# A two-layer hybrid decoder step on one core: the norm's first step on ScalarE, mixer B's affine step on GpSimd, eight logit tiles in place of ten

## The chip, the core and the metric

The kernel runs on one core of a Trainium2 chip. A core has five engines with a queue of instructions each: TensorE (PE, with its weight loads shown apart as PEld), VectorE (DVE), ScalarE (ACT), GpSimd (POOL) and SyncE (SP), which here issues the DMA transfers. The engines wait for one another by semaphores; within a queue the order is fixed when the program is built. The metric is the device time of one execution in microseconds (us); less is better.

## What is computed

One inference step of a decoder trunk of two layers, for a prompt of 2048 tokens (model width 1024) and for eight sample tokens that attend to 2048 cached tokens each. All is in float32. Layer 0 runs a chunked spatial gate (mixer A) and stick-breaking attention (mixer B, 8 heads of 64); layer 1 runs sparse softmax attention with 256 selected keys per query and a relative bias (mixer C, 8 query heads, 2 key heads) and causal pooling (mixer D). Each layer has one input projection, one output projection and a norm behind it:

```python
def stick_breaking(q, k, v, q_pos, k_pos):
    z = jnp.einsum('bqhd,bkhd->bhqk', q.astype(jnp.float32), k.astype(jnp.float32)) * HEAD_DIM ** -0.5
    mask = k_pos[None, :] < q_pos[:, None]
    log_keep = jnp.where(mask, jax.nn.log_sigmoid(-z), 0.0)
    later = lax.cumsum(log_keep, axis=3, reverse=True) - log_keep
    att = jnp.where(mask, jnp.exp(jax.nn.log_sigmoid(z) + later), 0.0)
    return jnp.einsum('bhqk,bkhd->bqhd', att, v.astype(jnp.float32)).astype(v.dtype)
...
    logits = jnp.where(valid[:, :, None, None, :], logits + bias, -jnp.inf)
    p = jax.nn.softmax(logits, axis=-1)
    o = jnp.einsum('bqgrk,bqkgd->bqgrd', p, v_sel)
...
def _layer_norm(x, g, b):
    return (_standardize(x) * g.astype(jnp.float32) + b.astype(jnp.float32)).astype(x.dtype)
...
def post_norm(x, h, w_o, g, b):
    return _layer_norm(DN_ALPHA * x + jnp.einsum('bte,ed->btd', h, w_o), g, b)
```

The outputs are both token groups behind layer 1, and the new keys, values and pooling rows of both layers.

## The kernel before

**Tiling.** The prompt is cut into four blocks of 512 tokens (i, or the block's number), each block into four tiles of 128 tokens, one per partition. Keys come in pieces of 512 columns (TB). A projection is computed in three float32r matmuls of split operands: wh and wl are a weight's high and low halves (L475 on ScalarE, L478 on GpSimd or VectorE), xh and xl those of the input (L462 on ScalarE, L468 on VectorE or GpSimd).

**Mixer B** goes block by block: for a pair of heads m, a key piece s and each head a of the pair, `b_logits` makes four tiles of 128 queries by up to 512 keys: the logits z (L839, TensorE), the keep probability by a sigmoid, the mask on the diagonal piece (L849, GpSimd), and a running product over the keys from the right (L853, a scan on VectorE). `b_values` transposes them (L876), copies them (L877, ScalarE) and multiplies with the values (L885). While the last block (i = 3) runs beside mixer C, the sigmoid is written as 0.5 + 0.5 tanh (`self.exp`: mixer C's exps use ScalarE too): L843 is the tanh, L844 the affine step. These are 4 pairs x 4 pieces x 2 heads x 4 tiles = 128 steps, 104 of them 128x512 and 24 of fewer columns on the diagonal.

**The norm** (`ln`) follows the output projection of each block and layer: statistics and a reciprocal square root by small steps on VectorE (rs_t at L492 to L495 is part of it), ln_nb = -mean x ln_rs at L1017, and then for each half c of the 1024 columns and each of four token tiles three steps in place on the rows xres: x ln_rs + ln_nb (L1026), times g (L1027, GpSimd, lng), plus b (L1028, VectorE, lnb). A norm of a block has eight such triples of 128x512; that of the sample tokens has two of 8x512. Behind layer 0 the rows are stored, loaded again, transposed on TensorE (ps_x), and split into xh and xl for layer 1's projection (pp at L549 to L551).

**Mixer C** goes by query tiles j = 0 to 15; tile j has j + 1 key tiles of 128, that is 1 to 4 pieces. For each head `c_logits` loads a bias tile nm and adds the mask to it (L1568, GpSimd), multiplies (z_c, L1581) and evicts each piece with mask and row maximum (L1583, VectorE) into a tile zt of the pool "z"; L1587 takes the maximum of the pieces (nmax). `c_values` takes the exp (L1599, ScalarE), transposes (L1612), copies (L1614, ScalarE) and, for two heads together, multiplies with the values (av_c, L1626). A counter z_free lets c_logits begin a piece only when a tile is free; L1626's loop frees two at a time. The tokens' selection (tk_ names) runs on VectorE, ScalarE and GpSimd. The sample tokens' work (names with s_) runs in the background.

**Stages.** `run` opens three sets of tile pools, one after the other. In the trace they take 0 to 1310 us (layer 0 and most of mixer B), 1310 to 1990 us (mixer B's last block beside mixer C's first tiles; here self.exp holds), and 1990 to 2925 us (mixer C's tiles 8 to 15 and three output projections with their norms); the last norms fill the tail to 2963 us. `BUFS_C` sizes the pools of the last stage.

**What sets the order.** The program is first written as streams that are woven together, and then the class `Order` plans it anew: a list scheduler over all instructions, with a cost for each by engine, operation and shape, with semaphore and transfer delays, and with the number of tiles of each tag as a limit. It plans three times (by program order, then by the latest start in the plan before) and keeps the plan with the shortest estimate. So an edit to an engine or a buffer count re-orders every queue, not only the lines edited.

## Time and profile before

| | us |
|---|---|
| median of three runs | 2964.18 |
| lowest, highest | 2955.64, 2974.54 |
| the profiled execution | 2964.62 |
| its span in the trace | 2962.9 |
| TensorE busy in the span | 2747.0 |
| VectorE busy | 2163.9 |
| ScalarE busy | 1561.7 |
| GpSimd busy | 1112.2 |

TensorE's granted clock over the whole span is 0.96 of full speed; full speed is 2.4 GHz and the lower level 1.2 GHz. The engines work beside each other, so the busy times do not add up to the span. An idle time in the rows below is that of the engine named, just before the instruction, with the engine and line that released it.

### The profile page before, as it was taken

To read this page: it belongs to the slowest core of one execution; us is meant where nothing else is said; L and a number is where in the kernel's file an instruction comes from. 1 tells how busy PE (TensorE), PEld (TensorE's weight loads), DVE (VectorE), ACT (ScalarE), POOL (GpSimd) and SP (SyncE) were. 2 spreads that over 40 slices of the span, in tenths; PEclk is the share of its full clock that TensorE was granted. 3 is DMA by queue.
4 is the path that set the end of the run, shared out by engine and by line. 5 is a ranking of instruction groups with operands and counts; after the bars stand their busy time and mean duration, and the time that the engine had idled before them with its cause. 6 is when DMAs were issued, how large, how long until landed. Compare 5 with 4: busy or idle time off the path is not lost. (4 is left out here: it accounts for less than half of the span.)

```text
span 2962.9 us, 52295 instructions
## 1 busy us (share of the span) xinstructions
PE 2747.0 (93%) x17490; PEld 2184.8 (74%) x17490; DVE 2163.9 (73%) x5493; ACT 1561.7 (53%) x3148; POOL 1112.2 (38%) x1172
## 2 busy tenths in 40 slices
PE   7998999989999999979799999998899998998995
PEld 6886777767767777768477677777777887887885
DVE  2366557856775887438988998897897778887766
ACT  2433333334444344435466677784577666675852
POOL 2323335423324543242433422335422555344342
PEclk9999999999999999989899999999999999998998
DMA  7566865776585668453665455425655565675452
GB/s 220 166 175 195 266 191 186 239 227 205 172 245 165 216 184 292 147 155 111 194 173 152 140 144 146 122 79 146 189 164 157 171 190 161 213 216 172 129 185 67
DMA packets 536594, 523.51 MB, mean 177 GB/s; under 512 B 43184, under 2 KB 408905, under 8 KB 536288
## 3 DMA queue, kind: packets, MB, share of 16 engines
q1 hardware_dynamic: 526439, 484.29, 55.1%
q0 software_dynamic: 9856, 35.66, 3.9%
q8 instruction: 138, 2.26, 0.3%
q14 instruction: 161, 1.31, 0.1%
HBM read 430.27 MB, written 89.73 MB: 176 GB/s over the span
## 5 line engine op out<-in xcount | busy, mean ns | idle before, releaser
L478 POOL TENSOR_TENSOR wl<-wr,wh 128x512 fp32r<-128x512 f32 x260 | 410.7, 1580 | 967.8 <-ACT wh L475 810.5
L549 PE MATMUL pp<-xh,wh 128*128 128x512 f32 (+1 forms) x1536 | 635.6, 417 | 10.2 <-DVE q_hl L468 6.1
L550 PE MATMUL pp<-xl,wh 128*128 128x512 f32 (+1 forms) x1536 | 616.4, 402 | 9.6 <-DVE rs_t L494 8.2
L551 PE MATMUL pp<-xh,wl 128*128 128x512 f32 (+1 forms) x1536 | 616.0, 401 | 1.0 <-DVE wl L478 1.0
L475 ACT CAST wh<-wr 128x1024 fp32r<-128x1024 f32 x260 | 269.9, 1038 | 386.5 <-PE pp L550 198.7
L478 DVE TENSOR_TENSOR wl<-wr,wh 128x512 fp32r<-128x512 f32 x260 | 219.0, 843 | 210.7 <-ACT wh L475 190.0
L549 PEld LDWEIGHTS pp<-xh,wh 128*128 128x128 f32 (+1 forms) x1536 | 288.6, 189 | 95.7 <-issue 27.8
L550 PEld LDWEIGHTS pp<-xl,wh 128*128 128x128 f32 (+1 forms) x1536 | 290.6, 189 | 68.6 <-issue 9.3
L551 PEld LDWEIGHTS pp<-xh,wl 128*128 128x128 f32 (+1 forms) x1536 | 289.6, 189 | 63.9 <-issue 4.6
L944 PE MATMUL pp_o<-wh,oh 128*128 128x256 f32 x1008 | 301.0, 300 | 17.9 <-ACT oh L462 11.8
L946 PE MATMUL pp_o<-wh,ol 128*128 128x256 f32 x1008 | 291.5, 293 | 2.6 <-POOL ol L468 2.6
L945 PE MATMUL pp_o<-wl,oh 128*128 128x256 f32 x1008 | 293.2, 292 | 0.0
L853 DVE TENSOR_TENSOR_SCAN P<-P,bfst 128x512 f32<-128x512 f32 x192 | 268.5, 1408 | 22.3 <-ACT P L846 21.8
L877 ACT COPY P<-ps_p 128x512 f32<-128x512 f32 (+1 forms) x320 | 166.0, 523 | 189.2 <-PE ps_p L876 180.4
L1581 PE MATMUL z_c<-ksc,qc 128*128 128x512 f32 (+3 forms) x816 | 222.0, 355 | 32.6 <-DVE mx L1583 27.3
L1599 ACT ACTIVATE zt<-zt,nmax 128x512 f32<-128x512 f32 (+3 forms) x320 | 209.0, 655 | 76.8 <-DVE nmax L1587 76.3
L1614 ACT COPY zt<-ps_pc 128x512 f32<-128x512 f32 (+3 forms) x320 | 164.1, 520 | 114.9 <-PE ps_pc L1612 113.3
L944 PEld LDWEIGHTS pp_o<-wh,oh 128*128 128x128 f32 x1008 | 198.1, 197 | 28.7 <-ACT oh L462 13.2
L1568 POOL TENSOR_TENSOR nm<-nm,mk 128x256 f32<-128x256 f32 (+1 forms) x128 | 92.7, 725 | 335.1 <-DMA nm<-bft 186.1
L839 PE MATMUL z<-ks,q 128*128 128x512 f32 (+3 forms) x640 | 194.0, 391 | 18.9 <-DMA ks<-ksc 10.8
L946 PEld LDWEIGHTS pp_o<-wh,ol 128*128 128x128 f32 x1008 | 197.1, 197 | 8.8 <-POOL ol L468 4.5
L945 PEld LDWEIGHTS pp_o<-wl,oh 128*128 128x128 f32 x1008 | 198.5, 197 | 5.2 <-issue 2.1
(456 smaller groups left out, 5861.2 us busy)
## 6 DMA issues: line engine op xcount, KB each, us to landing
pg<-cache_b_kv SPq DMA_DIRECT2D x256, 256.0 KB
wr<-w_in_even SPq DMA_DIRECT2D x112, 512.0 KB
wr<-w_in_odd SPq DMA_DIRECT2D x76, 512.0 KB
wr<-w_out SPq DMA_DIRECT2D x68, 512.0 KB
ks<-ksc SPq DMA_DIRECT2D x80, 256.0 KB
ksc<-kcs SPq DMA_DIRECT2D x80, 256.0 KB
q<-qsc SPq DMA_DIRECT2D x64, 256.0 KB
qc<-qcs SPq DMA_DIRECT2D x128, 128.0 KB
```

The source lines that it names most:

```text
L475: nc.scalar.copy(hi, raw)
L478: e.tensor_tensor(lo[:, c], raw[:, c], hi[:, c].bitcast(F32), op=OP.subtract)
L549: nc.tensor.matmul(ps[:m], wh[:, kt, :m], xh[kt], start=a, stop=False)
L550: nc.tensor.matmul(ps[:m], wh[:, kt, :m], xl[kt], start=False, stop=False)
L551: nc.tensor.matmul(ps[:m], wl[:, kt, :m], xh[kt], start=False, stop=b)
L839: nc.tensor.matmul(z[:, :n], q2[:, c, t * P:(t + 1) * P].bitcast(F32R), ks[:, :n].bitcast(F32R), start=c == 0, stop=c == 1)
L853: nc.vector.tensor_tensor_scan(r, r, r, initial=ini, op0=OP.mult, op1=OP.bypass)
L944: nc.tensor.matmul(ps[:, :256], oh[:, tt], wh[:, k], start=a, stop=False)
L945: nc.tensor.matmul(ps[:, :256], oh[:, tt], wl[:, k], start=False, stop=False)
L946: nc.tensor.matmul(ps[:, :256], ol[:, tt], wh[:, k], start=False, stop=b)
L1581: nc.tensor.matmul(z[:, :n], q2[:, c, jj % 2, :].bitcast(F32R), kk, start=c == 0, stop=c == 1)
L1599: nc.scalar.activation(zt, zt, AF.Exp, bias=nmx, accum_out=st["rs"][:, h, c:c + 1])
```

## The change

Three edits. `BUFS_C` gives mixer C's last phase eight logit tiles z where it had ten. The affine step behind the tanh (L844) goes from VectorE to GpSimd. The norm's first step (L1026) goes from VectorE to ScalarE, as an ACTIVATE of the identity with a scale and a bias per row, which computes the same.

```diff
@@ -37,7 +37,7 @@
 BUFS = {"tmp": 4, "tok": 4, "ot": 3, "hl": 1, "wr": 2}
 BUFS_A = {"P": 4, "q2": 3, "vs": 2}
 BUFS_M = {"P": 3, "q2": 2, "vs": 1, "z": 6, "kv": 2}
-BUFS_C = {"z": 10, "kv": 4}
+BUFS_C = {"z": 8, "kv": 4}
 KT = 8
 T = 2048
 TB = 512
@@ -841,7 +841,7 @@
             p = Ps[:, t]
             if self.exp:
                 nc.scalar.activation(p[:, :n], z[:, :n], AF.Tanh, scale=-0.0625)
-                nc.vector.tensor_scalar(p[:, :n], p[:, :n], 0.5, 0.5, op0=OP.mult, op1=OP.add)
+                nc.gpsimd.tensor_scalar(p[:, :n], p[:, :n], 0.5, 0.5, op0=OP.mult, op1=OP.add)
             else:
                 nc.scalar.activation(p[:, :n], z[:, :n], AF.Sigmoid, scale=-0.125)
             if diag:
@@ -1023,7 +1023,7 @@
             nc.sync.dma_start(b, self.bc(self.I["ln_b"][layer, cs], P))
             for t, y in enumerate(ys):
                 z = y[c]
-                nc.vector.tensor_scalar(z, z, rs[:n, t:t + 1], nb[:n, t:t + 1], op0=OP.mult, op1=OP.add)
+                nc.scalar.activation(z, z, AF.Identity, scale=rs[:n, t:t + 1], bias=nb[:n, t:t + 1])
                 nc.gpsimd.tensor_tensor(z, z, g[:n], op=OP.mult)
                 nc.vector.tensor_tensor(z, z, b[:n], op=OP.add)
             yield
```

In instructions that are 128 steps fewer on VectorE and more on GpSimd at L844, and 68 fewer on VectorE and more on ScalarE at L1026 (64 of 128x512, 4 of 8x512). TensorE's instructions are the same in number. The plan of every queue is new.

The first place is VectorE in the norm of block 2, layer 0: xres_15197 to xres_15203 are its four row tiles, rs_t and ln_rs of 8x1 belong to the sample tokens' norm, xl_16612 is the low half of the next projection's input. Before, on VectorE:

```order
L492 TENSOR_TENSOR rs_t_16553<-ln_rs_16551 8x1
L1026 TENSOR_SCALAR xres_15199<-xres_15199,ln_rs_16486,ln_nb_16504 128x512
L493 TENSOR_TENSOR rs_t_16553<-rs_t_16553,rs_a_16552 8x1
L1026 TENSOR_SCALAR xres_15201<-xres_15201,ln_rs_16486,ln_nb_16504 128x512
L494 TENSOR_SCALAR rs_t_16553<-rs_t_16553 8x1
L1028 TENSOR_TENSOR xres_15199<-xres_15199,lnb_16507 128x512
L495 TENSOR_TENSOR ln_rs_16551<-ln_rs_16551,rs_t_16553 8x1
L1026 TENSOR_SCALAR xres_15203<-xres_15203,ln_rs_16486,ln_nb_16504 128x512
L492 TENSOR_TENSOR rs_t_16553<-ln_rs_16551 8x1
L1028 TENSOR_TENSOR xres_15201<-xres_15201,lnb_16507 128x512
L493 TENSOR_TENSOR rs_t_16553<-rs_t_16553,rs_a_16552 8x1
L468 TENSOR_TENSOR xl_16612<-ps_x_16606,xh_16611 128x512
```

The last three of eight L1026 and two adds stand here ahead of xl.

Now, on VectorE, the same stretch up to the same xl (tk_ names belong to mixer C's selection):

```order
L1309 TENSOR_SCALAR tk_sd_16896<-tk_b_16898 128x1
L1382 TENSOR_SCALAR tk_b1_15964<-tk_tn_15706 128x1
L493 TENSOR_TENSOR rs_t_16553<-rs_t_16553,rs_a_16552 8x1
L1028 TENSOR_TENSOR xres_15199<-xres_15199,lnb_16507 128x512
L494 TENSOR_SCALAR rs_t_16553<-rs_t_16553 8x1
L1310 TENSOR_TENSOR tk_sd_16896<-tk_sd_16896,tk_a_16897 128x1
L495 TENSOR_TENSOR ln_rs_16551<-ln_rs_16551,rs_t_16553 8x1
L1028 TENSOR_TENSOR xres_15201<-xres_15201,lnb_16507 128x512
L492 TENSOR_TENSOR rs_t_16553<-ln_rs_16551 8x1
L1321 TENSOR_SCALAR tk_tt_16908<-tk_sd_16896,tkc_165,tk_mv_16895 128x1
L493 TENSOR_TENSOR rs_t_16553<-rs_t_16553,rs_a_16552 8x1
L468 TENSOR_TENSOR xl_16612<-ps_x_16606,xh_16611 128x512
```

The adds are left; small steps of the selection have moved in between them.

And on ScalarE, where the first steps now stand; xh_16611 is the high half that xl_16612 needs, P a copy of mixer B, zt an exp of mixer C:

```order
L1026 ACTIVATE xres_15197<-xres_15197,ln_nb_16504,ln_rs_16486 128x512
L1026 ACTIVATE xres_15199<-xres_15199,ln_nb_16504,ln_rs_16486 128x512
L1026 ACTIVATE xres_15201<-xres_15201,ln_nb_16504,ln_rs_16486 128x512
L877 COPY P_16195<-ps_p_16615 128x4x128
L1026 ACTIVATE xres_15203<-xres_15203,ln_nb_16504,ln_rs_16486 128x512
L462 CAST xh_16611<-ps_x_16606 128x512
L1649 ACTIVATE c_sum_16628<-ps_rb_16623 128x256
L1327 ACTIVATE mk_16645,tk_ss_16910<-ix_16644,tk_tt_16908 128x512
L1599 ACTIVATE zt_16639,rs_16330<-zt_16639,nmax_16782 128x256
```

The eight L1026 left VectorE's queue ahead of xl; on ScalarE all eight stand ahead of xh.

The second place is GpSimd ahead of the same norm: wl are low halves of weights, nm bias tiles of mixer C, P the probability tiles of mixer B. Before, on GpSimd:

```order
L478 TENSOR_TENSOR wl_16095<-wr_16092,wh_16094 128x512
L1568 TENSOR_TENSOR nm_16336<-nm_16336,mk_15227 128x256
L478 TENSOR_TENSOR wl_16149<-wr_16146,wh_16148 128x512
L1568 TENSOR_TENSOR nm_16635<-nm_16635,mk_15227 128x256
L1568 TENSOR_TENSOR nm_16787<-nm_16787,mk_15227 128x256
L478 TENSOR_TENSOR wl_16386<-wr_16383,wh_16385 128x144
L478 TENSOR_TENSOR wl_16455<-wr_16452,wh_16454 128x512
L1568 TENSOR_TENSOR nm_16973<-nm_16973,mk_15227 128x256
L1286 AFFINE_SELECT ix_16644<-ix_16644 128x128
L1568 TENSOR_TENSOR nm_17078<-nm_17078,mk_15227 128x256
```

Weight halves and bias tiles alternate. Now, on GpSimd:

```order
L478 TENSOR_TENSOR wl_16095<-wr_16092,wh_16094 128x512
L478 TENSOR_TENSOR wl_16149<-wr_16146,wh_16148 128x512
L844 TENSOR_SCALAR P_16195<-P_16195 128x512 x3
L1568 TENSOR_TENSOR nm_16635<-nm_16635,mk_15227 128x256
L844 TENSOR_SCALAR P_16195<-P_16195 128x512
L478 TENSOR_TENSOR wl_16386<-wr_16383,wh_16385 128x144
L478 TENSOR_TENSOR wl_16455<-wr_16452,wh_16454 128x512
L844 TENSOR_SCALAR P_16320<-P_16320 128x512 x4
L1568 TENSOR_TENSOR nm_16787<-nm_16787,mk_15227 128x256
L1568 TENSOR_TENSOR nm_16973<-nm_16973,mk_15227 128x256
L1286 AFFINE_SELECT ix_16644<-ix_16644 128x128
```

The affine steps stand in groups of up to four between the weight halves and the bias tiles.

The third place is VectorE in tile 15 of mixer C, with heads of four pieces: mx8_40839 and nmax_40951 belong to one head, zt_40968 (zt_41004 in the new program) and mx8_40967 to the first head of the next pair. Before, on VectorE:

```order
L1583 ISA zt_40922,mx8_40839<-z_c_40947,nm_40836 128x256
L1583 ISA mx8_40839 128x1
L1583 ISA zt_40968,mx8_40967<-z_c_40969,mk_36724 128x512
L1583 ISA mx8_40967 128x1
L1587 TENSOR_REDUCE nmax_40951<-mx8_40839 128x1
L949 SCALAR_TENSOR_TENSOR xres_40532<-xres_40532,pp_o_40682 128x256
```

The first eviction of the next pair (zt_40968) stands ahead of nmax. Now, on VectorE:

```order
L949 SCALAR_TENSOR_TENSOR xres_40534<-xres_40534,pp_o_40686 128x256
L1587 TENSOR_REDUCE nmax_40951<-mx8_40839 128x1
L949 SCALAR_TENSOR_TENSOR xres_40528<-xres_40528,pp_o_40794 128x256
L1639 TENSOR_REDUCE ri_41152<-rs_40274 128x4
L1012 BN_STATS bn12_41578<-xres_40528 128x6
L1640 RECIPROCAL ri_41152<-ri_41152 128x4
L949 SCALAR_TENSOR_TENSOR xres_40530<-xres_40530,pp_o_40795 128x256
L1012 BN_STATS bn12_41582<-xres_40530 128x6
L949 SCALAR_TENSOR_TENSOR xres_40534<-xres_40534,pp_o_40934 128x256
L478 TENSOR_TENSOR wl_40992<-wr_40989,wh_40991 128x512
L949 SCALAR_TENSOR_TENSOR xres_40532<-xres_40532,pp_o_40933 128x256
L1583 ISA zt_41004,mx8_40967<-z_c_41005,mk_36724 128x512
```

The next pair's first eviction (zt_41004) now stands ten rows behind nmax, after steps of the output projection (pp_o) and of the norm's statistics.

## Rows read from the trace of the kernel before

**Rows 1.** The page's part 1: busy time of each engine, its share of the span and its number of instructions.
```profile
PE 2747.0 (93%) x17490; PEld 2184.8 (74%) x17490; DVE 2163.9 (73%) x5493; ACT 1561.7 (53%) x3148; POOL 1112.2 (38%) x1172
```

**Rows 2.** Busy time by stretch (windows view), two of the three stages: bounds in us, length, then busy us (and instructions) of TensorE, its weight loads, VectorE, ScalarE and GpSimd; then TensorE's granted clock, the DMA engines' share and GB/s.
```profile
1310.00:1990.00 680.00, 625.09 (x3959) 470.26 (x3959) 583.51 (x1772) 444.33 (x974) 229.06 (x287) 0.96 0.51 143
1990.00:2925.00 935.00, 861.51 (x6648) 747.35 (x6650) 733.39 (x2300) 604.75 (x1224) 398.16 (x393) 0.94 0.56 167
```

**Rows 3.** The same view for five stretches in which a norm's steps stand close together.
```profile
1420.00:1450.00 30.00, 14.39 (x52) 7.90 (x53) 25.81 (x71) 6.24 (x14) 23.25 (x20) 0.60 0.41 129
2115.00:2160.00 45.00, 35.09 (x217) 25.92 (x213) 41.01 (x123) 23.97 (x57) 16.37 (x14) 0.77 0.69 211
2485.00:2530.00 45.00, 39.14 (x327) 33.97 (x326) 41.88 (x94) 30.20 (x63) 23.04 (x19) 0.91 0.60 198
2670.00:2715.00 45.00, 34.61 (x263) 31.13 (x261) 39.58 (x98) 23.11 (x49) 27.94 (x29) 0.81 0.56 184
2818.00:2850.00 32.00, 28.38 (x242) 23.12 (x239) 29.92 (x64) 18.87 (x44) 23.50 (x19) 0.89 0.64 205
```

**Rows 4.** The timeline from 1418 to 1452 us, the third norm of the first layer (block 2): start, duration (of several instructions in a row, with their count at the end), engine, line, operation, tiles and shapes; in brackets the idle time of the engine before it and what ended that.
```profile
1424.82 0.15 DVE L1017 SCALAR_TENSOR_TENSOR ln_nb<-ln_mv,ln_rs 128x4 f32<-128x4 f32 x1
...
1425.63 16.96 POOL L1027 TENSOR_TENSOR xres<-xres,lng 128x512 f32<-128x512 f32 x8 [1.26 <-DVE rs_t L492]
...
1427.47 1.21 DVE L493 TENSOR_TENSOR rs_t<-rs_t,rs_a 8x1 f32<-8x1 f32 x1
...
1428.53 0.59 ACT L462 CAST xh<-ps_x 128x512 fp32r<-128x512 f32 x1
1428.61 0.53 DVE L1026 TENSOR_SCALAR xres<-xres,ln_rs,ln_nb 128x512 f32<-128x512 f32 x1
...
1437.36 0.67 DVE L468 TENSOR_TENSOR xl<-ps_x,xh 128x512 fp32r<-128x512 f32 x1
...
1438.08 0.64 PE L550 MATMUL pp<-xl,wh 128*36 128x512 f32 x1 [8.16 <-DVE rs_t L494]
```

**Rows 5.** Timelines from 2117 to 2146 us and from 2670 to 2712 us, rows of TensorE that waited; and as the last row the waits of TensorE from 2818 to 2850 us (line waited at, what it waited for: us in total, times, longest).
```profile
2121.85 0.48 PE L1581 MATMUL z_c<-ksc,qc 128*128 128x256 f32 x2 [0.81 <-DVE xres L1026]
...
2134.18 0.80 PE L1271 MATMUL z_i<-kid,qi 128*128 128x512 f32 x1 [5.59 <-DVE mx L1583]
...
2687.63 1.87 PE L2112 MATMUL ps_so<-s_lg,s_pg 128*128 128x8 f32 x8 [6.36 <-DVE s_acc L2115]
...
PE z_c L1581 <- DVE mx L1583: 3.2, 2, 2.3
```

**Rows 6.** Groups by line, engine, operation and form over the whole run: count, busy us in all, mean ns of one, idle time of the engine just before them and what ended it. The last row is the same from 1310 to 1990 us, with the forms of a line taken together.
```profile
L853 DVE TENSOR_TENSOR_SCAN P<-P,bfst 128x512 f32<-128x512 f32 x192 | 268.5, 1408 | 22.3 <-ACT P L846 21.8
...
L1027 POOL TENSOR_TENSOR xres<-xres,lng 128x512 f32<-128x512 f32 x64 | 103.1, 1629 | 58.0 <-DVE xres L1026 48.9 <-DMA lng<-ln_g 5.2 <-DVE nmax L1587 1.5
...
L1026 DVE TENSOR_SCALAR xres<-xres,ln_rs,ln_nb 128x512 f32<-128x512 f32 x64 | 63.3, 1021 | 0.1
...
L1028 DVE TENSOR_TENSOR xres<-xres,lnb 128x512 f32<-128x512 f32 x64 | 60.5, 956 | 1.7 <-POOL xres L1027 1.7
...
L844 DVE TENSOR_SCALAR P<-P 128x512 f32<-128x512 f32 (+3 forms) x128 | 56.6, 444 | 11.4 <-ACT P L843 10.6
```

**Rows 7.** The same groups by form, whole run, of ScalarE: a function of a tile alone (L658), two with a per-row operand (L1599, the exp of mixer C, and L1390), and a copy out of PSUM (L1614).
```profile
L1599 ACT ACTIVATE zt<-zt,nmax 128x512 f32<-128x512 f32 x224 | 160.5, 719 | 65.3 <-DVE nmax L1587 65.0 <-issue 0.2
...
L1614 ACT COPY zt<-ps_pc 128x512 f32<-128x512 f32 x224 | 129.3, 585 | 92.0 <-PE ps_pc L1612 90.6
...
L658 ACT ACTIVATE g_s<-g_s 128x512 f32<-128x512 f32 x32 | 20.2, 633 | 15.0 <-DVE g_s L657 14.8
...
L1390 ACT ACTIVATE r<-ix,tk_b 128x512 f32<-128x512 f32 x28 | 19.6, 723 | 8.1 <-DVE tk_m L1392 7.4 <-DVE tk_b L1382 0.6
```

**Rows 8.** The same groups by form, whole run, of GpSimd: an affine select over eight rows of 512 elements.
```profile
L1745 POOL TENSOR_SCALAR_AFFINE_SELECT s_own<-s_own 8x512 f32<-8x512 f32 x1 | 0.6, 603 | 0.0
```

**Rows 9.** Waits from 1310 to 1990 us: engine, line, what it waited for: us in total, times, longest.
```profile
POOL wl L478 <- ACT wh L475: 107.0, 29, 13.2
POOL nm L1568 <- DMA nm<-bft: 92.1, 25, 12.6
...
PE z_c L1581 <- DVE mx L1583: 9.4, 5, 5.1
...
PE z L839 <- DVE mx L1583: 4.6, 5, 1.6
```

**Rows 10.** The timeline from 2922 us to the end, the last norms: columns as in group 4.
```profile
2929.53 0.16 DVE L1017 SCALAR_TENSOR_TENSOR ln_nb<-ln_mv,ln_rs 128x3 f32<-128x3 f32 x1
...
2934.46 4.71 POOL L1027 TENSOR_TENSOR xres<-xres,lng 128x512 f32<-128x512 f32 x3 [0.55 <-DVE rs_t L493]
...
2944.16 0.67 DVE L1028 TENSOR_TENSOR xres<-xres,lnb 128x512 f32<-128x512 f32 x1
...
2953.64 2.49 POOL L1027 TENSOR_TENSOR xres<-xres,lng 128x512 f32<-128x512 f32 x2 [5.18 <-DMA lng<-ln_g]
```

**Rows 11.** VectorE's eviction of mixer C's logits: by form over the whole run (first row), and in the waits of VectorE from 2400 to 2925 us (second row).
```profile
L1583 DVE CUSTOM_DVE_ANT_0 zt<-z_c,mk 128x512 f32<-128x512 f32 x168 | 114.8, 686 | 35.1 <-PE z_c L1581 23.9 <-PE av_c L1626 4.6 <-DVEq L1413 4.4
...
DVE zt L1583 <- PE av_c L1626: 4.8, 6, 2.0
```

## The prediction

> **What bounds the kernel now.** I read the page first. TensorE is busy for 2747.0 of 2962.9 us and VectorE for 2163.9 [rows 1], so what a change can win is mostly TensorE's idle 216 us, and only where VectorE, ScalarE or GpSimd end that idling. Next, the busy time by stage [rows 2]: the change touches the 680 us in which mixer B's last block and mixer C run side by side (1310 to 1990 us: TensorE idle 54.9 us, VectorE busy 583.5, GpSimd 229.1), mixer C's last phase (TensorE idle 73.5 us of 935), and the tail, the 38 us behind 2925. Then the same view around the norm's bursts [rows 3]: five stretches of 197 us hold 45.4 us of idle TensorE, and the granted clock in them is 0.60, 0.77, 0.91, 0.81 and 0.89. A burst is sixteen 128x512 steps on VectorE and eight on GpSimd.
>
> The burst at 1425 us shows what TensorE waits for [rows 4]. ln_nb, from which the burst starts, is written at 1424.82. GpSimd's eight multiplies fill 16.96 us. An eight-row step of another norm, on one element per row, takes 1.21 us. The split xl that TensorE needs, whose hi half ScalarE began at 1428.53, runs on VectorE only at 1437.36, behind all eight L1026 steps and three of the adds, and TensorE stands idle for 8.16 us. Other bursts do the same [rows 5]: 0.81 and 5.59 us around 2121 and 2134; 6.36 us at 2687; 3.2 us from 2818 to 2850. Together 24.1 us.
>
> **The change, part by part.**
>
> 1. The norm's first step. VectorE loses 64 steps of 128x512 and four of eight rows. Alone one takes 0.53 us [rows 4]; their mean is 1.021 us, 63.3 us in all [rows 6]. GpSimd's multiplies average 1.629 and the last add 0.956, though in the tail two multiplies take 2.49, so 1.25 each, and the add 0.67 [rows 6, 10]. So the two engines hold each other up inside a burst. ScalarE gets the steps. No row shows an ACTIVATE with two per-row operands: with none, 128x512 from SBUF takes 0.633 us, with one 0.723 [rows 7], so a second one like the first gives 0.81; the bounds are 0.72 (it costs nothing) and 0.90 (it costs double). Eight are 6.5 us of ScalarE, which is busy for 605 us of the last phase's 935 [rows 2].
> For the burst at 1425 us: the planned order leaves xl behind the three adds alone and puts ScalarE's xh behind all eight new steps. xh can start 6.5 us after ln_nb, and xl ends at about 6.5 + 0.59 + 0.67 = 7.8 us, where it now ends 1437.36 + 0.67 - 1424.82 = 13.2 us after. The 8.16 us wait would shrink to some 2.7, by two thirds. Elsewhere ScalarE's new steps delay exps and copies, and part of the waiting only changes its name. I take back 15 of the 24.1 us; bounds 5 and 24.
> The clock. At the lower of its two levels (1.2 in place of 2.4 GHz) for a share of a stretch, TensorE's work there takes twice the time. The five granted clocks [rows 3] mean 24.0 + 20.7 + 8.1 + 17.1 + 7.0 = 77 us at the low level; with TensorE busy for about 0.8 of that, half of 62 us, 31 us, is lost. The stretch with the longest stand-still has the lowest clock. I take a quarter, 8 us; bounds 0 and 20.
> The tail. From ln_nb at 2929.53 to the end of the last add of three rows at 2944.83 pass 15.3 us [rows 10], with GpSimd's three multiplies stretched to 4.71 us. With the first step on an idle ScalarE it is 0.81 + 6 x 1.25 + 0.67 = 9.0 us. The stores, the last row's load of g and its steps hang on that end. So up to 6 us; I take 5. The last multiplies wait 5.18 us for the load of g [rows 10], not for L1026, which has run before; there the move to ScalarE is covered by that load, and without the cover would cost 0.81 - 0.53 = 0.3 us.
> The Trainium skill, "ScalarE: Activation LUTs", Rules for kernel authors, speaks against this edit: adds and multiplies belong on VectorE. By the lone step it agrees with the rows (0.53 against 0.81), and 68 steps would cost 19 us more if each stood on the path, which would make the sum 2964; the rows of the burst show VectorE's queue to be what TensorE waits for, so I follow them.
>
> 2. The affine step behind tanh. VectorE loses 128 steps (104 of them 128x512), 56.6 us [rows 6], all inside the stage of 680 us. GpSimd gets them. No row shows a full-width one-input arithmetic step there: an affine select over 512 elements takes 0.603 [rows 8], a two-input step 1.25 [rows 10]. I take 0.75, nearest the one-input row; bounds 0.60 and 1.25. That is 88 us (70 to 147) on an engine that is idle for 451 us of the stage. It comes in groups of up to four steps, each waiting for its tanh, and GpSimd's queue holds the weight halves (wl) and mixer C's bias tiles (nm) behind them; today GpSimd waits for those inputs itself, 107.0 and 92.1 us [rows 9], so a microsecond more is mostly covered. Without that cover, 32 groups each late by one step of 0.75 cost 24 us. I take 3 us.
> What VectorE wins is less than 56.6 us. The scans that follow (1.408 us on average over the run) and other steps with two SBUF inputs collide with GpSimd's reads: the eight-row step that took 1.21 us is one [rows 4]. Bounds: nothing lost, or 88 us of new GpSimd work blocking it all along. If half of the 128 new steps hold VectorE up for as long as the burst holds up L1026 (1.021 - 0.53 = 0.49 us), 31 us return. TensorE's waits for VectorE in this stage outside the burst are 9.4 + 4.6 = 14.0 us [rows 9]; I take back a fifth, 3 us; bounds -5 and 10.
> The Trainium skill, "SBUF — State Buffer", Who interferes with whom, states that GpSimd and VectorE share a port pair under an exclusive lock, and whoever comes second is fully blocked. The 1.21 us step agrees. By it every new GpSimd step can block a scan whole, and the 3 us become a loss; this is the third rival.
>
> 3. Eight logit tiles. A pair of heads with 2048 keys holds four tiles each, so from tile 12 on eight are one pair and no tile is left for the next. In the planned order VectorE now evicts the next pair's first logits before the maximum of the present pair; with eight it does so only after the first values matmuls. A gap can be as long as an eviction, an exp and a copy, 0.686 + 0.719 + 0.585 = 2.0 us [rows 7, 11], at 15 places (four in each of tiles 12 to 15, the last has no successor): 30 us, if nothing fills it. The order has output-projection matmuls there, and TensorE is at 92% of this phase, so I take 8 us; bounds 0 and 30. The 4 KB of each partition given back are used by nothing.
>
> **Sum.** -15 - 8 - 5 + 3 - 3 + 8 = -20 us. The profiled execution took 2964.6 us (its span and 1.7 us around it), which is the median's 2964.2 within half a microsecond: **2944.6 us**, say 2945, 0.7% below.
>
> **The rivals.**
> - The waits change their name. The eight ACTIVATEs stand ahead of xh and of exps, TensorE waits for ScalarE where it waited for VectorE, and the clock falls as before. For it: 6.5 us of new ScalarE work in a 13 us burst, and ScalarE already at 65%. Against: xl's path shortens even so. It leaves the tail's 5 us, +3, -3 and +8: 2967 us.
> - The burst dissolves: all 24 us of waits, 20 of the clock, 6 of the tail and 10 in the mixed stage, with buffers free: 2964.6 - 60 = 2905 us. For it: VectorE and GpSimd block each other visibly. Against: GpSimd's multiplies still need 8 x 1.25 us a burst.
> - GpSimd blocks the scans. Each of the 128 steps takes 1.25 us and holds VectorE up for as long: 160 us against 56.6 saved, so its 583.5 us become 687. The highest share that it reaches in the bursts is 0.935 (29.92 of 32 us [rows 3]); at that share the stage needs 735 us, 55 more than now. It decides from the point where a new step holds VectorE up for 0.85 us (0.935 x 680 - 527 = 109 us, over 128). For it: that step of 1.21 us. Against: scans have run beside GpSimd's 229 us with a mean of 1.408. The time: 2964.6 - 28 + 8 + 55 = 3000 us.
> - The tiles run out. The 30 us come whole, and each stand-still brings the clock down for 3 us, another 15 to 20 us: 2945 - 8 + 48 = 2985.
>
> **Chances.** Forecast (2925 to 2957) 0.42, waits renamed 0.28, burst dissolved 0.13, scans blocked 0.09, tiles run out 0.08. A change of 1% is about the least that a measurement of this kernel tells from none; it lies at 2935 and 2994. Faster: the burst dissolved and a third of the forecast, 0.27. Slower: three quarters of the scans and a third of the tiles, with a little for a new order of every queue that none of these covers, 0.12. Same: 0.61. The range 2908 to 2990 leaves out half of the dissolved burst, most of the blocked scans and a part of the tiles, about 0.17; the forecast's own is 2925 to 2957.
>
> **What would show it.** Right: no L1026 on VectorE, L1028 near 0.7 us, GpSimd's eight multiplies of the burst in 11 to 13 us in place of 17, the wait of pp for the split under 4 us, and the granted clock of the burst above 0.75; tail 32 to 34 us. ScalarE's L1026 at 0.8 us. GpSimd's L844 at 0.7 to 0.9 us with scans under 1.4. In the last phase, evictions waiting for av_c by more than today's 4.8 us [rows 11]. Wrong: L844 above 1.2 us with VectorE still over 570 us in the stage; TensorE waiting for xh or zt by more than 20 us; TensorE waiting at z_c in the last phase by 20 us more than now. Those would make it the third, first or fourth rival.

## The result

The changed kernel takes 2945.93 us (median of 17 runs, 2938.73 to 2956.16), the kernel before 2964.32 us (17 runs, 2951.75 to 2974.90). The ratio is 0.9942, with a 95% interval of 0.9929 to 0.9955: 0.58% faster, where 0.7% and 2945 us were forecast. The profiled execution of each lies near its median, so the two traces can be compared.

The page of the changed kernel, its span and its part 1 (as in [rows 1]):

```profile
span 2944.2 us, 52298 instructions
...
PE 2738.7 (93%) x17490; PEld 2176.2 (74%) x17490; DVE 2121.0 (72%) x5297; ACT 1607.0 (55%) x3216; POOL 1202.9 (41%) x1300
```

VectorE's busy time fell by 43 us, although the steps taken from it had durations of 63.3 and 56.6 us in all before [rows 6]. Part of the difference is steps that stayed and became longer: without L1026 and L844, VectorE's durations add up to 2382.5 us before and 2436.6 us now, 54 us more. The rest is that durations of neighbouring steps overlap in the trace, and busy time counts an overlap once. Two stretches of the windows view (as in [rows 2]):

```profile
1310.00:1990.00 680.00, 631.51 (x3984) 476.27 (x3984) 569.96 (x1644) 453.65 (x992) 317.34 (x408) 0.95 0.50 141
1990.00:2925.00 935.00, 859.73 (x6680) 741.35 (x6679) 730.74 (x2289) 627.66 (x1253) 408.20 (x398) 0.95 0.55 168
```

In the mixed stage VectorE's busy time fell by only 13.5 us of 583.5. The stretches of the norms, moved by the few microseconds that the norms now come earlier (as in [rows 3]):

```profile
1411.00:1441.00 30.00, 15.37 (x53) 8.83 (x54) 28.87 (x86) 14.50 (x30) 18.90 (x23) 0.56 0.50 148
2112.00:2157.00 45.00, 33.89 (x186) 24.27 (x186) 36.60 (x117) 31.21 (x68) 16.22 (x14) 0.70 0.64 199
2485.00:2530.00 45.00, 38.90 (x317) 32.84 (x317) 40.15 (x99) 35.54 (x71) 21.35 (x18) 0.96 0.69 234
2665.00:2710.00 45.00, 39.66 (x324) 34.29 (x323) 41.91 (x109) 32.53 (x65) 31.28 (x31) 0.92 0.70 224
2805.00:2837.00 32.00, 27.30 (x225) 22.37 (x221) 27.64 (x62) 23.56 (x49) 23.07 (x17) 0.95 0.66 220
```

The granted clock is 0.56 and 0.70 in the first two (0.60 and 0.77 before) and 0.96, 0.92 and 0.95 in the last three (0.91, 0.81 and 0.89 before). The time at the lower level in the five is 26.4 + 27.0 + 3.6 + 7.2 + 3.2 = 67 us; it was 77.

The timeline of the third norm, the burst on which the prediction was worked out (as in [rows 4]):

```profile
1417.21 0.14 DVE L1017 SCALAR_TENSOR_TENSOR ln_nb<-ln_mv,ln_rs 128x4 f32<-128x4 f32 x1
...
1417.39 5.04 ACT L1026 ACTIVATE xres<-xres,ln_nb,ln_rs 128x512 f32<-128x512 f32 x7 [0.26 <-DVE ln_nb L1017]
...
1418.28 11.60 POOL L1027 TENSOR_TENSOR xres<-xres,lng 128x512 f32<-128x512 f32 x8 [0.76 <-ACT xres L1026]
...
1422.68 1.18 DVE L493 TENSOR_TENSOR rs_t<-rs_t,rs_a 8x1 f32<-8x1 f32 x1
...
1423.52 0.56 ACT L462 CAST xh<-ps_x 128x512 fp32r<-128x512 f32 x1
...
1428.60 0.67 DVE L468 TENSOR_TENSOR xl<-ps_x,xh 128x512 fp32r<-128x512 f32 x1
...
1429.32 0.64 PE L550 MATMUL pp<-xl,wh 128*36 128x512 f32 x1 [4.53 <-DVE rs_t L494]
...
1437.33 0.45 PE L525 MATMUL ps_x<-idf,xc 128*128 128x128 f32 x1 [6.08 <-DMA xc<-x]
```

ScalarE writes seven first steps in 5.04 us (the eighth follows behind a copy), GpSimd's eight multiplies take 11.60 us (16.96 before), and TensorE's wait for the low half xl is 4.53 us (8.16 before). The small step L493 still takes 1.18 us beside GpSimd; it is one of seven small steps between ln_nb and xl that take 1.03 to 1.24 us each. So xl ends 1428.60 + 0.67 - 1417.21 = 12.1 us behind the start of ln_nb, where it took 13.2 us before. A second wait, for the rows that the norm stored and that are loaded again (xc), is now the longest, 6.08 us. It isn't new: in these 30 us TensorE's waits for xc were 7.1 us before, in two, and are 8.5 us now, in three. Groups by form over the whole run (as in [rows 6]; L1026 is on ScalarE, L844 on GpSimd):

```profile
L853 DVE TENSOR_TENSOR_SCAN P<-P,bfst 128x512 f32<-128x512 f32 x192 | 273.4, 1432 | 36.8 <-ACT P L846 24.7 <-POOL P L844 9.5 <-DVEq L1413 2.3
...
L1027 POOL TENSOR_TENSOR xres<-xres,lng 128x512 f32<-128x512 f32 x64 | 98.3, 1562 | 45.1 <-ACT xres L1026 38.1 <-DMA lng<-ln_g 5.0 <-PE pp L551 1.8
...
L844 POOL TENSOR_SCALAR P<-P 128x512 f32<-128x512 f32 x104 | 83.0, 800 | 101.5 <-ACT P L843 94.9 <-DMA qc<-qcs 3.5 <-DMA wr<-w_in_odd 2.8
...
L1028 DVE TENSOR_TENSOR xres<-xres,lnb 128x512 f32<-128x512 f32 x64 | 71.1, 1125 | 7.3 <-POOL xres L1027 7.2
...
L1026 ACT ACTIVATE xres<-xres,ln_nb,ln_rs 128x512 f32<-128x512 f32 x64 | 48.6, 808 | 8.1 <-DVE ln_nb L1017 8.1
```

L1026 takes 0.808 us on ScalarE and L844 0.800 us on GpSimd; 0.81 and 0.75 were taken. The add L1028, which was to fall to 0.7, rose from 0.956 to 1.125 us.

**Where the time came from.** Three marks divide the span: the first tanh L843 (mixer B's last block begins), the last tanh, and the last av_c matmul L1626 (mixer C ends). They stand in the view of one source line: count, shortest/median/longest in ns, first and last start in us, forms (the last av_c matmul by its weight load, on PEld). The kernel before:

```profile
L843 ACT ACTIVATE P<-z x128: 250/598/637, 1311.6 to 1983.8; 128x512 f32<-128x512 f32 x104, 128x128 f32<-128x128 f32 x8, 128x256 f32<-128x256 f32 x8, 128x384 f32<-128x384 f32 x8
...
L1626 PEld LDWEIGHTS av_c<-zt,vsc x2176: 132/137/232, 1347.6 to 2925.1; 128*64 128x64 f32 x198
...
L1028 DVE TENSOR_TENSOR xres<-xres,lnb x64: 660/679/1774, 557.9 to 2956.6; 128x512 f32<-128x512 f32 x64
```

The changed kernel:

```profile
L843 ACT ACTIVATE P<-z x128: 277/598/652, 1302.4 to 1978.9; 128x512 f32<-128x512 f32 x104, 128x128 f32<-128x128 f32 x8, 128x256 f32<-128x256 f32 x8, 128x384 f32<-128x384 f32 x8
...
L1626 PEld LDWEIGHTS av_c<-zt,vsc x2176: 132/137/232, 1340.1 to 2911.3; 128*64 128x64 f32 x198
...
L1028 DVE TENSOR_TENSOR xres<-xres,lnb x64: 671/977/1797, 556.3 to 2937.5; 128x512 f32<-128x512 f32 x64
...
L844 POOL TENSOR_SCALAR P<-P x128: 294/623/1582, 1303.7 to 1979.6; 128x512 f32<-128x512 f32 x104, 128x128 f32<-128x128 f32 x8, 128x256 f32<-128x256 f32 x8, 128x384 f32<-128x384 f32 x8
```

Before the first tanh the change gains 9.2 us (1311.6 to 1302.4), up to the last tanh it loses 4.3, up to the last av_c it gains 8.9, and behind that 4.9: 18.7 us of span. One of the two large pieces is where the prediction had put nothing: the stage before 1310 us holds the first two norms, and of the three edits only the norm's step has instructions there. The order of that stage is new too, so the edit's share of the 9.2 us is read below from runs with the order held.

### The profile page after: what moved, and what is told of

Its sections match the earlier page's. It is cut to its first block, busy times and chain, and to the rows that moved or that the text cites. A ratio compares the mean times of both kernels' runs of the same rounds, so it can differ in the third digit from the quotient of the medians.

```text
span 2944.2 us, 52298 instructions
## 1 busy us (share of the span) xinstructions
PE 2738.7 (93%) x17490; PEld 2176.2 (74%) x17490; DVE 2121.0 (72%) x5297; ACT 1607.0 (55%) x3216; POOL 1202.9 (41%) x1300
## 5 line engine op out<-in xcount | busy, mean ns | idle before, releaser
L853 DVE TENSOR_TENSOR_SCAN P<-P,bfst 128x512 f32<-128x512 f32 x192 | 273.4, 1432 | 36.8 <-ACT P L846 24.7
L1599 ACT ACTIVATE zt<-zt,nmax 128x512 f32<-128x512 f32 (+3 forms) x320 | 208.6, 654 | 63.0 <-DVE nmax L1587 60.0
L1614 ACT COPY zt<-ps_pc 128x512 f32<-128x512 f32 (+3 forms) x320 | 163.4, 518 | 101.2 <-PE ps_pc L1612 97.6
L1568 POOL TENSOR_TENSOR nm<-nm,mk 128x256 f32<-128x256 f32 (+1 forms) x128 | 101.3, 792 | 273.7 <-DMA nm<-bft 160.6
L1327 ACT ACTIVATE mk<-ix,tk_tn 128x384 int8<-128x384 f32 (+13 forms) x140 | 183.5, 1311 | 45.6 <-DVE tk_tn L1377 29.5
```

Of the source, the lines that this page charges most:

```text
L853: nc.vector.tensor_tensor_scan(r, r, r, initial=ini, op0=OP.mult, op1=OP.bypass)
L1599: nc.scalar.activation(zt, zt, AF.Exp, bias=nmx, accum_out=st["rs"][:, h, c:c + 1])
```

## The experiments

Any edit makes the planner write a new order, so the runs are of three kinds: single edits with a new plan (e1 to e3), the same program with a new plan (e4, e5, e9, e10), and edits with the order held still (d1, d2, d3, d5, d7). Each ratio is to the kernel before on the same chip, over five rounds, with its 95% interval.

**e1: the norm's step alone.**

```diff
-                nc.vector.tensor_scalar(z, z, rs[:n, t:t + 1], nb[:n, t:t + 1], op0=OP.mult, op1=OP.add)
+                nc.scalar.activation(z, z, AF.Identity, scale=rs[:n, t:t + 1], bias=nb[:n, t:t + 1])
```

> Only the norm's first step moves to ScalarE; the affine step stays on VectorE and the logit tiles stay ten. The prediction's own terms for this edit (waits -15, clock -8, tail -5) give 28 us less than before, a ratio of 0.9906. Rival one, relief of VectorE as such (its removed busy time is 63 us here, 57 us for the affine step): about half of the 18 us that the three edits gave, 9 to 10 us, ratio 0.997. Rival two, the new order of the queues as such: anything within 10 us of before, with no clear relation to the steps removed. In the trace: L1026 on ScalarE at 0.81 us, the tail behind the last av_c matmul some 5 us shorter in the first theory.

Measured: 2950.01 us, ratio 0.9962 [0.9951, 0.9974]: 11 us. That is near the first rival's 9 to 10 us, at the edge of the second's, and under half of the prediction's 28.

**e2: the affine step alone.**

```diff
-                nc.vector.tensor_scalar(p[:, :n], p[:, :n], 0.5, 0.5, op0=OP.mult, op1=OP.add)
+                nc.gpsimd.tensor_scalar(p[:, :n], p[:, :n], 0.5, 0.5, op0=OP.mult, op1=OP.add)
```

> Only the affine step behind the tanh moves to GpSimd. The prediction's terms (+3 for GpSimd's queue, -3 for VectorE) give 0, ratio 1.000, within 3 us. Relief of VectorE as such: 8 to 9 us less, ratio 0.997. GpSimd blocking the scans: 10 us or more slower, with L853 above 1.5 us on average. In the trace: L844 at 0.80 us, 128 steps of about 100 us on GpSimd between 1310 and 1990 us.

Measured: 2984.04 us, ratio 1.0076 [1.0062, 1.0091]: 23 us slower. By its time this looked like the prediction's third rival, blocked scans; but the scans averaged 1.43 us over the run, under the 1.5 us that blocking was to show.

**e3: eight logit tiles alone.**

```diff
-BUFS_C = {"z": 10, "kv": 4}
+BUFS_C = {"z": 8, "kv": 4}
```

> Only the logit tiles of mixer C's last phase go from ten to eight. The prediction's term is 8 us slower than before, ratio 1.0027 (bounds 0 and 30 us). Rival: the planner fills the gaps with output-projection matmuls and the time doesn't move, ratio 1.000 within 3 us, or the other order is even better. In the trace: VectorE's L1583 waits for av_c by more than the 4.8 us of before from 2400 to 2925 us; if TensorE's waits at z_c in that stretch don't grow, the rival holds.

Measured: 2978.44 us, ratio 1.0062 [1.0048, 1.0077]: 18 us slower.

The three add up to 30 us slower, while together they are 17 us faster. So they can't be added, or something else moves with them.

**e4: no edit, a nudged planner.** Two constants of the planner move together: the semaphore delay SEM and DMA_END, the time that it adds behind a transfer. Both are numbers of the plan alone.

```diff
-    SEM, DMA_START, DMA_END, RATE = 150, 700, 1500, 280.0
+    SEM, DMA_START, DMA_END, RATE = 152, 700, 1520, 280.0
```

> None of the three edits: only the planner's semaphore delay goes from 150 to 152 ns, so that every queue gets another order of the same instructions. It shows how much a new order alone can do. If the gain of the change is that of the steps moved, this stays within 5 us of before (ratio 0.998 to 1.002). If a new order alone does as much as the change, it moves by 10 us or more, either way, and single edits can't be read without it.

Measured: 2984.91 us, ratio 1.0081 [1.0065, 1.0097]: 24 us slower with not one instruction changed. A new order alone does as much as any edit here, and e1 to e3 can't be read as prices of their edits.

**d1 and d2: one step moved, the order of before kept.** The planner is told that the moved steps are still on VectorE, at VectorE's cost; afterwards they are taken out of its queue and put into the other engine's by their planned start. d1 (d2 marks L844 in the same way):

```diff
+                nc.scalar.activation(z, z, AF.Identity, scale=rs[:n, t:t + 1], bias=nb[:n, t:t + 1]); self.moved.append(self.tc.nc.cur_bb.bb.instructions[-1].name)
...
+def put(self, begun):
+    for n, e in sorted(self.moved.items(), key=lambda x: begun[x[0]]):
+        self.order["DVE"].remove(n)
+        o = self.order[e]
+        at = next((k for k, m in enumerate(o) if begun[m] > begun[n]), len(o))
...
+        o.insert(at, n)
```

> The norm's first step runs on ScalarE, but the planner plans as if it were still on VectorE, at VectorE's cost; its instructions are then taken out of VectorE's queue and set into ScalarE's where their planned start lies. Every other instruction keeps the place that it has before. So only the step itself is moved. If the gain comes from the steps moved (waits behind the bursts, the tail), this gains 11 us or more against before, ratio 0.990 to 0.996. If it comes from the new order, it stays within 5 us of before, ratio 0.998 to 1.002. ScalarE blocking exps and copies in a place not planned for it: a few us slower.

> The affine step runs on GpSimd, all other instructions in the order of before; the steps are set into GpSimd's queue where their planned start lies. With the affine step alone and a new plan the time rose by 23 us. If the step itself costs that (GpSimd's queue, blocked scans), this is 15 to 25 us slower than before, ratio 1.005 to 1.008. If the new order cost it, this lies within 5 us of before, ratio 0.998 to 1.002, as the prediction's term of 0 says.

Measured: d1 2950.91 us, ratio 0.9981 [0.9964, 0.9997]; d2 2963.19 us, ratio 1.0015 [1.0004, 1.0027]. In the order of before, the norm's step is worth 6 us (1 to 11) and the affine step costs 4; d1 lies in the band that was set for a gain that comes from the order. If the two add up, both steps in the old order come to 0.9981 x 1.0015 = 0.9996, next to nothing; that program was not run. So 18 of e2's 23 us were the new order, and GpSimd doesn't block the scans by anything near the third rival's price. The scans L853 of the mixed stage in the view of one source line, before and in d2:

```profile
L853 DVE TENSOR_TENSOR_SCAN P<-P,bfst x96: 1234/1274/2147, 1341.0 to 1988.7; 128x512 f32<-128x512 f32 x96
```

```profile
L853 DVE TENSOR_TENSOR_SCAN P<-P,bfst x96: 1252/1280/2330, 1341.0 to 1983.3; 128x512 f32<-128x512 f32 x96
```

The median hardly moves (1274 and 1280 ns); the longest have grown, and with them the mean, from 1.312 to 1.368 us.

**d3: ten tiles in the order of eight.** The program is woven and planned as for eight tiles, the pool has ten.

```diff
-        free = {g: max(self.tiles[t].tag_meta.bufs for t in ts) for g, ts in self.tags.items()}
+        free = {g: 8 if n == 10 else n for g, ts in self.tags.items() for n in [max(self.tiles[t].tag_meta.bufs for t in ts)]}
...
-            self.width, self.z_free = width, bufs["z"]
+            self.width, self.z_free = width, min(bufs["z"], 8)
```

> Mixer C's last phase has ten logit tiles again, but the program is woven and planned as for eight, so the order of every queue is that of the kernel with eight tiles alone (which took 17 us more than before); only the waits for a tile are eased. If those waits cost the 17 us, this comes back to before, ratio 1.000. If the order did, it stays near 1.006.

Measured: 2969.83 us, ratio 1.0042 [1.0028, 1.0057]. The order keeps 12 of e3's 18 us. What the tiles themselves cost is the difference, 0.2% or 6 us, and the two intervals overlap. VectorE's waits for av_c from 2400 us to the last av_c, in e3:

```profile
DVE zt L1583 <- PE av_c L1626: 8.6, 9, 1.7
```

In d3 no such wait is listed in that stretch. So the tiles do run out, for 8.6 us of VectorE's time. TensorE's waits at z_c, which e3 was to tell its rival by, did not grow; from 2400 to 2900 us, before and then e3:

```profile
PE z_c L1581 <- DVE mx L1583: 15.0, 10, 3.6
```

```profile
PE z_c L1581 <- DVE mx L1583: 13.0, 12, 4.7
```

That is the rival's sign in the trace, though the time did move: the waits for a tile don't show at z_c, and the larger part of e3's time is its order.

**d5 and d7: the new order kept, steps put back.** The reverse of d1 and d2: the planner is told that the steps run on ScalarE and GpSimd, at their costs there, and they run on VectorE. d5 puts both back, d7 the affine step alone.

```diff
+                nc.vector.tensor_scalar(p[:, :n], p[:, :n], 0.5, 0.5, op0=OP.mult, op1=OP.add); self.moved.append((self.tc.nc.cur_bb.bb.instructions[-1].name, "POOL"))
...
+                nc.vector.tensor_scalar(z, z, rs[:n, t:t + 1], nb[:n, t:t + 1], op0=OP.mult, op1=OP.add); self.moved.append((self.tc.nc.cur_bb.bb.instructions[-1].name, "ACT"))
```

> The changed kernel's order of all queues with its eight tiles, but both steps run on VectorE again, set into its queue where the plan had them start on ScalarE and GpSimd. If the steps moved give the gain, this loses it: 18 us or more over the changed kernel, ratio to before 1.000 or above. If the new order gives it, it keeps most: ratio 0.994 to 0.996. The prediction's terms for the two steps (-28 and 0) would put it at 2974 us, ratio 1.003.

> The changed kernel's order, with the affine step alone back on VectorE where the plan had it start on GpSimd; the norm's first step stays on ScalarE. With both back the time was 1.2% over the changed kernel. The prediction's terms (norm 28 us, affine 0) put this within 3 us of the changed kernel, ratio to before 0.993 to 0.996. If the relief of VectorE by the affine step counts in this order, it is 10 to 20 us over it, ratio 0.998 to 1.002.

Measured: d5 2977.80 us, ratio 1.0065 [1.0045, 1.0085]; d7 2951.00 us, ratio 0.9966 [0.9949, 0.9982]. The new order without the steps, with its eight tiles, is worse than the old one by 19 us; with the norm's step it gains 0.9966 / 1.0065 = 0.9902, 29 us (21 to 37), and with the affine step another 0.9942 / 0.9966 = 0.9976, 7 us (1 to 13). d5 and d7 were on different chips, each against the kernel before on its own. An order is made for its engines: each step is worth more in the order that was planned for it. Read from the other side, putting the steps back costs more in an order that has no room for them; the two readings can't be told apart.

**e5, e9, e10: more plans.** e9 is before with 148 ns; e5 and e10 are the changed kernel with 152 and 148 ns. DMA_END moves along as in e4, to 1520 with 152 and to 1480 with 148.

> All three edits, with the planner's semaphore delay at 152 ns, as in the run that nudged the kernel before and found it 0.8% slower than before. If the edits gain as such and an order adds its own luck, this is some 0.6% under that nudged kernel: ratio to before 1.000 to 1.004. If the order decides alone, it may lie anywhere from 0.994 to 1.010 with no relation to its partner.

> None of the edits, the planner's semaphore delay at 148 ns: a second new order of the kernel before. If the order of before is a lucky one, this is slower than it too, ratio 1.003 to 1.010; if the first nudge was an unlucky one, it lies within 0.3% of before.

> All three edits with the delay at 148 ns: the partner of the second nudge. If the edits gain as such, it is 0.3 to 0.9% under that partner, and the mean of the three pairs (150, 152, 148 ns) is the edits' own gain, about the forecast's 0.7%. If the order decides alone, the three pairs differ in sign.

| planner's delay | before | changed | changed / before |
|---|---|---|---|
| 150 ns | 1 | 0.9942 [0.9929, 0.9955] | 0.9942 |
| 152 ns | 1.0081 [1.0065, 1.0097] | 0.9993 [0.9984, 1.0003] | 0.9913 |
| 148 ns | 1.0068 [1.0048, 1.0088] | 1.0064 [1.0050, 1.0079] | 0.9996 |

The three pairs have one sign or none, with a mean of 0.995, 15 us; the pair with 148 ns misses the 0.3 to 0.9% that was expected of it. Equal programs in three orders spread over 0.8% (before) and 1.2% (changed), more than the change itself, so three pairs don't settle the mean. The order of before is the fastest of its three.

**The stages of all kernels**, from the same two lines of each trace, in us (one execution each):

| | to first tanh | to last tanh | to last av_c | to the end |
|---|---|---|---|---|
| before | 1311.6 | 672.2 | 941.3 | 37.8 |
| changed | 1302.4 | 676.5 | 932.4 | 32.9 |
| e1 norm | 1302.7 | 675.5 | 935.4 | 33.4 |
| d1 norm, old order | 1301.8 | 672.0 | 932.7 | 35.0 |
| e2 affine | 1312.5 | 678.0 | 957.8 | 38.3 |
| d2 affine, old order | 1308.4 | 671.3 | 949.0 | 38.2 |
| e3 eight tiles | 1309.0 | 673.8 | 949.2 | 38.0 |
| d3 ten tiles, order of eight | 1309.5 | 673.5 | 951.5 | 37.8 |
| d5 both back, new order | 1316.5 | 685.5 | 938.8 | 35.8 |
| d7 affine back, new order | 1299.5 | 681.1 | 928.8 | 32.7 |
| e4, e9 before, nudged | 1315.2, 1322.0 | 681.0, 686.2 | 943.7, 942.8 | 38.4, 36.5 |
| e5, e10 changed, nudged | 1305.7, 1314.3 | 675.0, 683.1 | 946.2, 942.1 | 32.4, 34.3 |

The rows of d1, d5 and d7 from which three lines of it come:

```profile
L843 ACT ACTIVATE P<-z x128: 253/597/642, 1301.8 to 1973.8; 128x512 f32<-128x512 f32 x104, 128x128 f32<-128x128 f32 x8, 128x256 f32<-128x256 f32 x8, 128x384 f32<-128x384 f32 x8
...
L1626 PEld LDWEIGHTS av_c<-zt,vsc x2176: 132/137/231, 1338.3 to 2906.5; 128*64 128x64 f32 x198
```

```profile
L843 ACT ACTIVATE P<-z x128: 278/598/652, 1316.5 to 2002.0; 128x512 f32<-128x512 f32 x104, 128x128 f32<-128x128 f32 x8, 128x256 f32<-128x256 f32 x8, 128x384 f32<-128x384 f32 x8
...
L1626 PEld LDWEIGHTS av_c<-zt,vsc x2176: 132/137/231, 1354.5 to 2940.8; 128*64 128x64 f32 x198
```

```profile
L843 ACT ACTIVATE P<-z x128: 277/597/658, 1299.5 to 1980.6; 128x512 f32<-128x512 f32 x104, 128x128 f32<-128x128 f32 x8, 128x256 f32<-128x256 f32 x8, 128x384 f32<-128x384 f32 x8
...
L1626 PEld LDWEIGHTS av_c<-zt,vsc x2176: 132/137/232, 1337.3 to 2909.4; 128*64 128x64 f32 x198
```

A stage that an edit doesn't touch and whose order is kept shows how far one execution can be trusted: to the first tanh before and d2 differ by 3.2 us, changed and d7 by 2.9; to the last av_c before and d2 by 7.7. Against that, the norm's step gains 9.8 us (before, d1), 17.0 (d5, d7), 9.5 (e4, e5) and 7.7 (e9, e10) ahead of the first tanh, and 2.2 to 6.0 in the tail (the nudged pairs with all three edits). Those two stages gain in every pair. In the two between, the pairs go from 10.0 us gained to 4.3 lost. The profiled executions lie from 8 us under their kernel's median (d1; d7 7 under) to 10 us over it (e9), so the rows of d1 and d7 overstate the step, and those of e9 and e10 show a gain that their medians don't.

The start of the first ln_nb (L1017), ahead of which the kernels of d1's and d7's pairs run the same instructions in the same order, takes part of that scatter out. The first two norms, before and d1, then d5 and d7:

```profile
L1017 DVE SCALAR_TENSOR_TENSOR ln_nb<-ln_mv,ln_rs x2: 153/157/161, 551.9 to 1082.1; 128x4 f32<-128x4 f32 x2
```

```profile
L1017 DVE SCALAR_TENSOR_TENSOR ln_nb<-ln_mv,ln_rs x2: 152/158/163, 550.2 to 1075.7; 128x4 f32<-128x4 f32 x2
```

```profile
L1017 DVE SCALAR_TENSOR_TENSOR ln_nb<-ln_mv,ln_rs x2: 152/157/162, 553.0 to 1082.5; 128x4 f32<-128x4 f32 x2
```

```profile
L1017 DVE SCALAR_TENSOR_TENSOR ln_nb<-ln_mv,ln_rs x2: 153/157/161, 548.6 to 1072.2; 128x4 f32<-128x4 f32 x2
```

d1 is 1.7 us and d7 4.4 us ahead before the first norm begins, and that can't be the step. From there to the first tanh d1 gains 8.1 us and d7 12.6, 4.7 and 5.9 of them up to the second norm's ln_nb. By the same two marks the change gains 10.5 us, e5 9.8 on e4 and e10 8.2 on e9, while d2 gains 3.1 on before and changed 1.7 on d7, where no edit has a step.

What the first norm does there can be seen in d1, which has the order of before. Windows of 540 to 640 us and of 0 to 1300 us, before and d1:

```profile
540.00:640.00 100.00, 86.84 (x419) 63.34 (x419) 79.93 (x119) 38.72 (x73) 32.79 (x34) 0.93 0.89 273
...
0.00:1300.00 1300.00, 1246.27 (x6779) 954.51 (x6780) 816.67 (x1348) 507.73 (x941) 460.07 (x475) 0.98 0.67 202
```

```profile
540.00:640.00 100.00, 89.02 (x432) 64.44 (x432) 74.76 (x108) 45.08 (x83) 33.83 (x33) 0.95 0.91 280
...
0.00:1300.00 1300.00, 1246.58 (x6819) 957.58 (x6819) 806.43 (x1336) 522.72 (x965) 468.34 (x482) 0.99 0.67 204
```

TensorE does 2.2 us more work in those 100 us, at a clock of 0.95 in place of 0.93; over 1300 us the clock is 0.99 in place of 0.98. TensorE's waits for xl from 540 to 640 us, before and then d1 (there with its remaining wait at ps_x):

```profile
PE ps_x L525 <- DVE xl L468: 2.5, 1, 2.5
...
PE pp L550 <- DVE xl L468: 1.3, 1, 1.3
```

```profile
PE pp L550 <- DVE xl L468: 1.9, 1, 1.9
...
PE ps_x L525 <- DMA xc<-x_prompt: 0.3, 1, 0.3
```

The wait of 2.5 us for xl is gone; the other rose from 1.3 to 1.9. Which waits make up the rest of the 8 to 13 us of the first two norms is not settled by these runs.

## Why the prediction was right, and where it was not

The total was right: 2945.9 against 2945, inside the forecast's own range of 2925 to 2957. Its terms were right in part.

- **The norm's step, -28 us** (waits -15, clock -8, tail -5). It measured 6 us in the old order, 29 in the new, 11 with a plan of its own. The direction holds, and that the steps moved are the cause is shown with the order held. The tail's term holds best: 37.8 to 32.9 us. The place was wrong for the rest: the sum went over the late bursts, where TensorE stood still, and took nothing for the two norms before 1310 us, where the gain is the steadiest, 8 to 13 us.
- **The burst that was worked out.** The path of xl was mis-sized. xl was to end 6.5 + 0.59 + 0.67 = 7.8 us behind ln_nb; it ended 12.1 us behind, and the wait was 4.53 us where 2.7 were worked out. xh came in time, at 1423.52. The sum had left out what still stood on VectorE ahead of xl: adds, and the small steps at 1.03 to 1.24 us each.
- **The clock, 8 us.** Not in the burst that was worked out: its clock fell to 0.56, above 0.75 was forecast. The wait for xl shrank to 4.53 us (under 4 forecast), and the waits for the stored rows, 8.5 us, stayed. Over the whole span, before and changed, the clock rose:

```profile
core 0: 2962.9 us, clock 0.960
```

```profile
core 0: 2944.2 us, clock 0.964
```

That is 2 x 0.040 x 2962.9 = 237 us at the lower level, and now 2 x 0.036 x 2944.2 = 212 us. Half of the 25 us, for a busy TensorE, is some 12 us. Over all runs the mean clock of before is 0.962 and that of the changed kernel 0.9645: some 16 us less at the lower level, half of which is 8. So the size was about right, the place again not.
- **VectorE and GpSimd in the burst.** The step that failed: "L1028 near 0.7 us". With L1026 gone, it is the add that stands against GpSimd's multiplies. Its shortest is 660 and 671 ns in both kernels, but its median went from 679 to 977. The runs with the order held show the same: its mean goes from 0.942 to 1.114 us (d5, d7) and from 0.956 to 1.256 (before, d1; there most of it in two adds). The multiplies fell only from 1.629 to 1.562 us on average; in the third norm they did as forecast (11.60 us, 11 to 13 forecast).
- **The affine step, 0 us.** +4 and -7 us in the two orders: 0 is between them. L844 at 0.800 us was within 0.7 to 0.9; the scans, forecast under 1.4 us, went to 1.432. The return of work to VectorE was seen (13.5 us of busy time won in the stage; 56.6 - 31 = 25.6 were worked out). With the affine step alone (d2), VectorE's other steps without L1026 add up to 665.9 us there and 643.6 before: 22 us came back, of 31 worked out.
- **Eight tiles, +8 us.** Some 6 us for the tiles, not told apart from nothing, and no longer wait of TensorE at z_c. In the changed kernel VectorE waits for av_c, from 2400 us to the last one, for

```profile
DVE zt L1583 <- PE av_c L1626: 8.7, 6, 3.3
```

which is more than the 4.8 us of before, as forecast [rows 11].
- **The step that was missing.** The prediction counted every edit's own cost and took the order as a carrier of it. A new order of the same instructions moves this kernel by 20 us and more (e4, e9). The orders gave a total near the sum of the terms; with 152 ns in the planner the same three edits lie within 0.1% of the kernel before. In the order of before the two steps together come to next to nothing, as far as d1 and d2 add up; the gain needs the order that was planned with them. The sum's agreement to one microsecond is luck; the range had to be as wide as it was for another reason than the one given.
- **The rivals.** That the waits change their name is seen in one place and in part: in the third norm the wait for xl fell by 3.6 us and the waits for xc rose by 1.4. The burst didn't dissolve. Blocked scans fall by d2. Tiles that run out at 30 us fall by d3.

## What to carry to other kernels

Where a planner orders the queues, measure how far a nudge of the planner alone moves the time before any edit's effect is believed, and compare edits in pairs under the same nudges or with the order held still. A step should be tried in the order that was planned for it and in the old one: the norm's step is worth 29 us in the one and 6 in the other. And when a step is moved away from an engine that collides with another, ask which of the steps that stay will meet the collision next.

## What was unexpected of the hardware

- The collision of VectorE and GpSimd isn't spread over the steps. L1028 takes 660 to 680 ns alone and, in the kernels before and after, up to 1797 ns when it meets a multiply; an eight-row step beside a multiply takes as long as a wide one, 1.18 us (1.21 in [rows 4]). GpSimd's L844 shows the same from the other side: median 623 ns over all its forms, longest 1582.
- A wait can be much longer than one multiply. In d1 an add begins just behind the start of the second of seven back-to-back multiplies and ends 0.56 us behind the last:

```profile
2118.20 8.64 POOL L1027 TENSOR_TENSOR xres<-xres,lng 128x512 f32<-128x512 f32 x7
...
2119.52 7.88 DVE L1028 TENSOR_TENSOR xres<-xres,lnb 128x512 f32<-128x512 f32 x1 [2.18 <-POOL xres L1027]
```

  Another add of d1 takes 9.7 us, again beside an almost unbroken row of GpSimd's steps. These two are 16 of the 19 us by which its 64 adds grew. Why most adds wait for one multiply and these for six is not shown.
- ScalarE is not touched by it: L1026 takes 0.808 us on average in the middle of GpSimd's multiplies. The Trainium skill, "SBUF — State Buffer", Who interferes with whom, says that ScalarE never waits for another engine's access; these rows agree.
- The same section of the Trainium skill says that VectorE and GpSimd share a port pair as an exclusive lock, and that whoever issues second is blocked for the other's whole instruction. The longest scans (2.33 us in d2) and the 1.8 us adds agree with one instruction waited for; d1's 7.88 us add goes beyond it. How often it happens is another matter: 128 new GpSimd steps left the scans' median where it was (1274 and 1280 ns).
